# Keys and values of the last two heads as pairs, normalization by quarters, and decode logits at other places

## The chip, the cores and the metric

The kernel runs on one core of one Trainium2 chip. The time is the device time of one execution in microseconds; the median of several runs is compared. The core's engines are TensorE (PE: matmuls and transposes, with its weight loads as PEld), VectorE (DVE), ScalarE (ACT), GpSimd (POOL) and SyncE (SP, which here only issues DMAs). PSUM is the memory that TensorE writes, SBUF the memory that every engine reads.

## The reference, cut to what matters

One inference step of a hybrid decoder layer. 16 meta tokens and 512 prompt tokens form one sequence; 8 samples of 4 new tokens each decode against 512 cached positions.

```
h = rmsnorm(x, g_pre)                                  # 560 rows of 2048
q, k, v, ga, cb, cc, ch, gc, ma, mc = split(h @ w_in)  # 12288 columns
a = stick_breaking(q, k, v) * silu(ga)                 # 8 heads of 128, strictly causal
c = cb * causal_conv(cc * ch, width 3) * silu(gc)
m = sigmoid(ma + b) * (a @ w_pa) + sigmoid(mc + b) * (c @ w_pc)
y = x + rmsnorm(m @ w_out, g_post)
# stick_breaking: z = q.k / sqrt(d) + b_h
#   A[t,s] = sigmoid(z[t,s]) * prod over s<j<t of (1 - sigmoid(z[t,j])); out = A @ v
```

All inputs and outputs are float32. Keys and values of the new tokens are outputs too.

## The kernel before, in words

**Precision.** Each float32 operand of a large product is split into two parts, `hi` (rounded to the fast format F32R) and `lo` (the rest). A product is three matmuls: hi x hi, hi x lo, lo x hi. ScalarE writes `hi` by a cast, VectorE writes `lo` by a subtraction (`w_split`, L253 and L254, for weight blocks of 128 x 1024).

**Layout.** Activations are held transposed, with channels on the partitions: `h_hi` and `h_lo` have 16 blocks of 128 channels by 560 tokens. The 560 tokens are two column halves of 280 (`HC`): a half begins with 8 meta tokens and goes on with 272 others (`HQ`).

**Start (L155 to L438).** The 560 rows arrive as five row tiles (`XT`): four of 128 rows, and one of 48 with the samples and 16 rows around them. Tile 2 has three pieces, of 16, 8 and 104 rows. `norm_stats` squares a whole tile on ScalarE with a sum (L211), then takes a logarithm and an exponential for 1/sqrt and refines it by a Newton step of five small operations. `norm_half` scales half a tile by that and by g (L220). g is broadcast over the partitions by 32 small matmuls (L187) and copied to SBUF by `g_copy` (L194). TensorE then transposes 128 x 128 blocks (L227), ScalarE casts them to `h_hi` (L235), and VectorE subtracts for `h_lo` (L239). Meanwhile the weights of the queries of heads 0 to 3 arrive in eight blocks; each is split by `q_high` (ScalarE, L323) and `q_low` (VectorE, L328). `q_chunk(c)` multiplies two channel blocks for the first 256 tokens as soon as they are there (L334), eight chunks in all; the other 296 tokens follow at once behind them (L438). Nearly everything in the start is pinned (`pin`), which keeps the order that the code has.

**Heads 0 to 3 (`head_now`).** Keys, values, and the queries of head 4 + h are projected one block of 128 columns at a time by `proj` and `gemm_into` (L269): two column halves, 16 channel blocks and three terms. `natural` transposes the result for the output. Then follows the head's attention.

**Heads 4 to 7 (`head_later`).** Keys and values are projected in the same way and put into DRAM for later.

**Pairs (`seven`, `pair`).** The remaining columns of w_in are computed in pairs of 128-column blocks, by a scheme of 7 block products instead of 8 (2 x 2 blocks: channel halves by column blocks; and channel halves by token halves). It needs sums of token blocks, `t_hi` and `t_lo`, which are made once from `h_hi` and `h_lo` behind head 7 (L959 to L979). Block (0, 1) of `h` is overwritten by such a sum, so that this step must come after the last direct projection. Four pairs of attention gates come first, then convolution pairs, then 16 pairs of merge gates.

**Decode attention (`decode_steps`).** This is a generator that is advanced by `dec_step` between other work. The first part is the logits: 16 units (half of the heads, sample) of four key pages each, 16 multiply-and-sum operations on VectorE per page (L795). The first `DEC1` = 6 units run beside the heads, the others beside the pairs, where `dec_group` counts finished pairs and says how many steps follow each. Then come the weights (exponentials), and then the values (L870), from pages loaded by POOL's queue.

**Order.** The order on each engine is fixed when the program is built, by a scheduler that follows a priority by code order and its own estimate of durations, except for what is pinned. Every engine then goes through its list in order. Weights come through SP's DMA queue, with five buffers (`wraw`) and three pairs of split buffers (`whl`).

Of the kernel before, what the change touches and what calls it, by code (L numbers as in the profile page):

```python
# [9 lines left out]
F32 = mybir.dt.float32  # L10
# [7 lines left out]
P = 128  # L18
# [21 lines left out]
      (((16, "p", 256), (8, "m", 8), (104, "p", 272)), ((0, 128, HM + 256),)),  # L40
# [20 lines left out]
def hybrid_step_kernel(  # L61
# [76 lines left out]
    def rstd_of(eng, out, ss, tmp, n, w=1, later=False, fix=lambda ins: ins):  # L138

        v, r, t = (tmp[:n, i * w:(i + 1) * w] for i in range(3))  # L140
        fix(act.activation(r, ss, AF.Ln, bias=eps_c[:n], scale=1.0 / D))
        fix(act.activation(r, r, AF.Exp, scale=-0.5))

        def newton(pin=lambda ins: ins):
            pin(eng.tensor_scalar(out=v, in0=ss, scalar1=1.0 / D, scalar2=EPS, op0=ALU.mult, op1=ALU.add))
            pin(eng.tensor_mul(t, r, r))
            pin(eng.tensor_mul(t, t, v))
            pin(eng.tensor_scalar(out=t, in0=t, scalar1=-0.5, scalar2=1.5, op0=ALU.mult, op1=ALU.add))
            pin(eng.tensor_mul(out, r, t))

        if not later:
            newton()
        return newton

# [3 lines left out]
    g_bc = sp.tile([P, D], F32, name="g_bc", bufs=1)  # L158
# [5 lines left out]
    act.preload_act_table_set(LNEXP)  # L164
    def warm_up(n):

        pt = t_ps()
        for _ in range(n):
            tc.keep_in_program_order(pe.matmul(pt, lhsT=neg_one, rhs=neg_one.unsqueeze(1).broadcast_to([P, 4, P]),  # L169
                                               start=True, stop=True))  # L170
# [3 lines left out]
    g_n = sp.tile([KD, P], F32, name="g_n", bufs=1)  # L174
    act.dma_start(g_n, g_pre.rearrange("o (k p) -> (o k) p", p=P))
    g_hl = sp.tile([KD, 2, P], F32R, name="g_hl", bufs=1)
    pick = sp.tile([KD, KD], F32R, name="pick", bufs=1)
    dve.tensor_copy(pick, ident[:KD, :KD])
    dve.tensor_copy(g_hl[:, 0, :], g_n)
    dve.tensor_sub(g_hl[:, 1, :], g_n, g_hl[:, 0, :].bitcast(F32))  # L180
    g_ps = []
    for c, mk in enumerate((mm_ps, mm_ps, mm_ps, z_ps)):
        pt = mk()
        for k in range(4):
            for n in range(2):
                tc.keep_in_program_order(
                    pe.matmul(pt[:, k * P:(k + 1) * P],  # L187
                              lhsT=pick[:, 4 * c + k:4 * c + k + 1].broadcast_to([KD, P]),
                              rhs=g_hl[:, n, :], start=(n == 0), stop=(n == 1)))
        g_ps.append(pt)  # L190

    def g_copy(c):
        copy = dve.tensor_copy if c < 2 else act.copy
        pin(copy(g_bc[:, c * 512:(c + 1) * 512], g_ps[c]))  # L194

    start_ps = cycle((z_ps, z_ps, z_ps, t_ps, o_ps))

    def x_load(i):
        n = sum(r[0] for r in XT[i][0])
        xt = sp.tile([P, D], F32, name="xt", bufs=3)[:n]  # L200
        load_x(xt, i)
        return i, n, xt

    def norm_stats(x, eng=dve):

        i, n, xt = x
        ss = sp.tile([P, 1], F32, name="ss", bufs=5)[:n]
        sq = sp.tile([P, D], F32, name="sq", bufs=1)[:n]
        rs = sp.tile([P, 1], F32, name="rs", bufs=5)[:n]
        tmp = sp.tile([P, 4], F32, name="rtmp", bufs=5)  # L210
        pin(act.activation(sq, xt, AF.Square, accum_out=ss))  # L211
        return (i, n, xt, rs), rstd_of(eng, rs, ss, tmp, n, later=True, fix=pin)

    def norm_half(c, x):


        i, n, xt, rs = x
        hn = sp.tile([P, D // 2], F32, name="hn", bufs=4)[:n]
        cs = slice(c * 1024, (c + 1) * 1024)
        pin(dve.scalar_tensor_tensor(out=hn, in0=xt[:, cs], scalar=rs, in1=g_bc[:n, cs],  # L220
                                     op0=ALU.mult, op1=ALU.mult))
        parts = []
        for kq in range(2):
            pt = next(start_ps)()
            pv = pt[:, :4 * n].rearrange("p (k t) -> p k t", t=n)
            for k in range(4):
                pin(pe.transpose(out=pv[:, k, :], in_=hn[:, (4 * kq + k) * P:(4 * kq + k + 1) * P],  # L227
                                 identity=ident[:n, :n]))
            k0 = 8 * c + 4 * kq
            for r0, r1, t0 in XT[i][1]:  # L230
                parts.append(((slice(None), slice(k0, k0 + 4), slice(t0, t0 + r1 - r0)), pv[:, :, r0:r1]))

        def highs():
            for dst, src in parts:
                pin(act.copy(h_hi[dst], src))  # L235
# [1311 lines left out]
```

## Time and profile before

| | |
|---|---|
| median of 3 runs | 1575.22 us (1573.78 to 1578.06) |
| the profiled execution | 1577.82 us, of which the profile's span is 1576.2 us |
| TensorE busy | 1561.8 us, 99% of the span |
| VectorE busy | 1260.8 us, 80% |
| ScalarE busy | 755.6 us, 48% |
| POOL busy | 236.3 us, 15% |
| DMA | 252.77 MB, mean 160 GB/s |

How to read the rows that follow. A row of the timeline or the chain begins with its start and its length in microseconds. "L334" is line 334 of the kernel. "mm<-h_hi,whi" names the tile written and the tiles read. "x72" is a count. A bracket at the end of a row gives the idle time of the engine before it and what ended it. Matmuls overlap, so the distance between the starts of two of them is the pace, and the length of one is longer than that.

### The profile page before, as it was taken

What the parts mean: (1) busy time and instruction counts of PE and PEld (TensorE: products, weight loads), DVE (VectorE), ACT (ScalarE), POOL (GpSimd) and SP (SyncE); (2) the same over time, 40 slices, a digit from 0 to 9 for tenths busy, and PEclk for the clock granted to TensorE, in tenths of its full rate; (3) what the DMA queues carried; (4) which work ended last, traced back from release to release, by engine and by line L of the source; (5) the groups of instructions that cost most, each with busy time, mean ns of one, the idle gap of its engine ahead of it and who ended that gap; (6) DMA issues with size and microseconds to landing.
All of it is one profiled execution on the core that took longest, in us unless ns stands there. A gap on an engine that the chain in (4) does not pass through costs nothing.

```text
span 1576.2 us, 32345 instructions
## 1 busy us (share of the span) xinstructions
PE 1561.8 (99%) x12172; PEld 1528.3 (97%) x12172; DVE 1260.8 (80%) x3567; ACT 755.6 (48%) x1345; POOL 236.3 (15%) x428
## 2 busy tenths in 40 slices
PE   9999999999999999999999999999999999999997
PEld 8999999999999999999999999898899999999997
DVE  6328999965799999999999996655678867877776
ACT  6335555434444443444444465444476734355563
POOL 1023333222011001011011113212100010000000
PEclk9999999999999999999999999999999999999999
DMA  8245655344563454545356547666596455433345
GB/s 250 73 143 175 178 165 178 117 125 130 170 189 113 144 153 143 149 135 162 106 173 187 157 143 224 185 207 219 166 292 188 140 186 167 153 107 95 101 140 189
DMA packets 300674, 252.77 MB, mean 160 GB/s; under 512 B 11521, under 2 KB 268613, under 8 KB 299701
## 3 DMA queue, kind: packets, MB, share of 16 engines
q1 hardware_dynamic: 272021, 160.45, 34.8%
q0 software_dynamic: 28368, 89.98, 17.2%
q8 instruction: 95, 1.56, 0.4%
q14 instruction: 62, 0.51, 0.1%
q10 hardware_dynamic: 128, 0.27, 0.1%
HBM read 217.95 MB, written 32.71 MB: 159 GB/s over the span
## 4 chain that ended last, share of the span: by engine, by line
PE 98%; DVE 1%; ACT 0%; issue 0%; DVEq 0%; ACTq 0%
PE mm L994 34%; PE mm L269 28%; PE o L994 25%; PE mm L334 2%; PE z L716 1%; PE o L728 1%; PE z L334 1%; PE tp L870 1%; PE z L634 1%; PE tp L519 0%; PE z L1332 0%; PE mm L187 0%; PE tp L169 0%; DVE x_n L1374 0%; PE z L227 0%; DVE hn L220 0%
## 5 line engine op out<-in xcount | busy, mean ns | idle before, releaser
L253 ACT CAST whi<-raw 128x1024 fp32r<-128x1024 f32 x247 | 259.3, 1051 | 323.1 <-PE mm L269 100.3
L254 DVE TENSOR_TENSOR wlo<-raw,whi 128x1024 fp32r<-128x1024 f32 x247 | 301.8, 1223 | 105.5 <-ACT whi L253 103.4
L994 PE MATMUL mm<-h_hi,whi 128*128 128x272 f32 (+1 forms) x1152 | 333.0, 289 | 0.0
L994 PE MATMUL mm<-h_lo,whi 128*128 128x272 f32 (+1 forms) x1152 | 332.7, 289 | 0.0
L994 PE MATMUL mm<-h_hi,wlo 128*128 128x272 f32 (+1 forms) x1152 | 331.7, 290 | 0.1
L994 PE MATMUL o<-t_hi,whi 128*128 128x272 f32 (+1 forms) x864 | 250.2, 290 | 0.0
L994 PE MATMUL o<-t_lo,whi 128*128 128x272 f32 (+1 forms) x864 | 249.9, 289 | 0.0
L994 PE MATMUL o<-t_hi,wlo 128*128 128x272 f32 (+1 forms) x864 | 249.8, 289 | 0.0
L795 DVE CUSTOM_DVE_ANT_0 junk<-kpage,qb 128x128 f32<-128x128 f32 x1024 | 245.3, 286 | 2.1 <-DMA qb<-q_scr 1.6
L994 PEld LDWEIGHTS mm<-h_hi,whi 128*128 128x128 f32 x1152 | 217.4, 189 | 6.7 <-ACT whi L253 3.4
L994 PEld LDWEIGHTS mm<-h_hi,wlo 128*128 128x128 f32 x1152 | 216.6, 189 | 1.3 <-DVE wlo L254 0.5
L994 PEld LDWEIGHTS mm<-h_lo,whi 128*128 128x128 f32 x1152 | 216.8, 188 | 0.1
L253 ACT CAST whi<-s 128x1024 fp32r<-128x1024 f32 x126 | 132.1, 1048 | 150.1 <-PE mm L994 54.2
L254 DVE TENSOR_TENSOR wlo<-s,whi 128x1024 fp32r<-128x1024 f32 x126 | 153.8, 1220 | 61.1 <-ACT whi L253 60.9
L269 PE MATMUL mm<-h_lo,whi 128*128 128x280 f32 (+1 forms) x640 | 187.6, 293 | 0.0
L269 PE MATMUL mm<-h_hi,wlo 128*128 128x280 f32 (+1 forms) x640 | 187.1, 293 | 0.0
L269 PE MATMUL mm<-h_hi,whi 128*128 128x280 f32 (+1 forms) x640 | 186.7, 292 | 0.0
L994 PEld LDWEIGHTS o<-t_hi,wlo 128*128 128x128 f32 x864 | 163.1, 189 | 0.7 <-DVE wlo L254 0.7
L994 PEld LDWEIGHTS o<-t_lo,whi 128*128 128x128 f32 x864 | 163.4, 189 | 0.0
L994 PEld LDWEIGHTS o<-t_hi,whi 128*128 128x128 f32 x864 | 163.0, 189 | 0.1
L269 PEld LDWEIGHTS mm<-h_lo,whi 128*128 128x128 f32 x640 | 120.3, 188 | 0.8
L269 PEld LDWEIGHTS mm<-h_hi,whi 128*128 128x128 f32 x640 | 120.5, 188 | 0.5
(462 smaller groups left out, 3166.7 us busy)
## 6 DMA issues: line engine op xcount, KB each, us to landing
raw<-in_w_in SPq DMA_DIRECT2D x192, 512.0 KB, 4.2
kpage<-in_cache_k POOLq DMA_DIRECT2D x64, 256.0 KB, 3.6
qb<-q_scr POOLq DMA_DIRECT2D x32, 512.0 KB, 5.7
vpage<-in_cache_v POOLq DMA_DIRECT2D x64, 256.0 KB, 5.9
raw<-in_w_out SPq DMA_DIRECT2D x32, 512.0 KB, 3.9
gate_scr<-g POOLq DMA_DIRECT2D x32, 272.0 KB, 3.3
gt<-gate_scr POOLq DMA_DIRECT2D x16, 544.0 KB, 4.6
raw<-in_w_pc SPq DMA_DIRECT2D x16, 512.0 KB, 4.5
```

Of the source, the lines that this page charges most:

```text
L253: act.copy(hi, x)
L254: low[0] = dve.tensor_sub(lo, x, hi.bitcast(F32))
L269: pe.matmul(o, lhsT=w, rhs=r[:, t0:t1], start=(k == 0 and n == 0), stop=(k == nk - 1 and n == 2))
L334: pin(pe.matmul(o, lhsT=l, rhs=r[:, k, t0:t1], start=(start and m == 0), stop=(stop and m == 2), skip_group_check=True))
L634: pe.matmul(zt[:m, c0:c0 + n], lhsT=l[:, s0:s0 + m], rhs=r[:, ts:ts + n], start=(c0 == 0 and i == 0), stop=(i == 2), skip_group_check=True)
L716: pe.matmul(o, lhsT=l, rhs=x, start=False, stop=(i == len(ops) - 1), skip_group_check=True)
L728: pe.matmul(ot[:, ts - NMETA:ts - NMETA + n], lhsT=l[:m, st, :], rhs=x[:m, c0:c0 + n], start=False, stop=(g == GROUPS[-1] and i == 2), ski ...
L795: dve.tensor_tensor_reduce(out=junk, in0=kt[:, h * P:(h + 1) * P], in1=qt[:, t, h * P:(h + 1) * P], scale=1.0, scalar=0.0, op0=ALU.mult, o ...
L870: pin(pe.matmul(po[32 * j:32 * (j + 1), :], lhsT=lhs, rhs=rhs, start=(pg == 0), stop=last and n >= len(vts) - 4, tile_position=(0, 32 * j) ...
L994: pe.matmul(o, lhsT=l[:, k, :], rhs=r, start=(start and k == 0 and m == 0), stop=(stop and k == 7 and m == 2), skip_group_check=True)
```

## The change

It has three parts.

1. **Keys and values of heads 6 and 7** are computed as two pairs by `seven`, on the full halves of 280 columns. The token sums become 280 wide and are made in steps between the four direct projections of heads 4 and 5 (`STEPS`), with VectorE's order pinned. Small copies of these two heads go to ScalarE.
2. **The start** is rewritten as a class `Rows`. Tile 0 is loaded in two halves. Squares, scalings, transposes and splits go by halves and quarters of a tile. g stays in PSUM, broadcast by 8 matmuls of 512 columns, and is read there by the scaling. Each chunk runs its three terms one after the other, with transposes of later quarters between them. All five tiles have buffers of their own. `q_low` runs on POOL. Tile 2 is loaded with its 104 rows as 96 and 8. There are more warm-up matmuls.
3. **Decode logits**: `DEC1` is 5; the key pages beside heads 0 to 3 are distributed by `PAGES`, one is ahead of head 0, and none is beside heads 4 and 5. The sample rows of the first four queries are transposed together. The small tables are loaded behind the query stores. The later decode steps come two pairs later.

```diff
-      (((16, "p", 256), (8, "m", 8), (104, "p", 272)), ((0, 128, HM + 256),)),
+      (((16, "p", 256), (8, "m", 8), (96, "p", 272), (8, "p", 368)), ((0, 128, HM + 256),)),
-DEC1 = 6
+DEC1 = 5
-WARM = 10
+WARM = 8
+SOLO = 6
...
+    g_hl = sp.tile([P, 2, 512], F32R, name="g_hl", bufs=1)
+    g_ps = [z_ps(), z_ps(), z_ps(), o_ps()]
+    for n in range(2):
+        for c, pt in enumerate(g_ps):
+            pin(pe.matmul(pt, lhsT=pick[:, c:c + 1].broadcast_to([P, P]), rhs=g_hl[:, n, :],
+                          start=(n == 0), stop=(n == 1)))
+    warm_up(7)
...
+    class Rows:                      # one row tile
+        def square(self, half):      # ScalarE, half a tile, sum into ss[:, half]
...
+        def square_on_vector(self, half):
...
+        def newton(self):            # 4 small VectorE operations
...
+        def scale(self, c):
+            self.hn[c] = hn = sp.tile([P, 512], F32, name="hn", bufs=5)[:self.n]
+            pin(dve.scalar_tensor_tensor(out=hn, in0=self.x[:, c * 512:(c + 1) * 512], scalar=self.rs,
+                                         in1=g_ps[c][:self.n], op0=ALU.mult, op1=ALU.mult))
+        def turn(self, c):           # 4 transposes into one of two PSUM tiles (flip)
...
-        pin(dve.tensor_sub(q_lo[c], q_raw[c], q_hi[c].bitcast(F32)))
+        pin(pool.tensor_sub(q_lo[c], q_raw[c], q_hi[c].bitcast(F32)))
...
+    x0.square(0)
+    x0.base()
+    x0.square(1)
+    x0.root()
+    x0.newton()
+    x1.square(0)
+    x0.scale(0)
+    x0.turn(0)
+    warm_up(9)
+    x1.square_on_vector(1)
+    q_high()
+    q_low()
+    x1.base()
+    x0.high(0)
+    x1.root()
+    x1.newton()
+    x1.scale(0)
+    x1.turn(0)
+    warm_up(2)
+    x0.low(0)
+    x0.scale(1)
+    x1.high(0)
+    x1.low(0)
...
+    q_chunk(0, ((x0.turn, 1), (x1.turn, 1),))
...
+    q_chunk(1, ((x0.turn, 2), (x1.turn, 2),))
+    x2.square(0)
+    x2.base()
+    x0.high(2)
+    x1.high(2)
...
+    q_high()
+    q_low()
+    q_load()
+    x2.square(1)
+    x2.root()
...
+    PAGES = ((2, 2, 2, 1), (1, 1, 2, 1), (1, 1, 1, 1), (1, 1, 1, 0))
...
+    def later_pair(c, h, qs=None, ready=None):
+        raws = [hp2.tile([P, T], F32, name="raw", bufs=2) for _ in range(2)]
+        seen = []
+        for m, half, b in pair(c + h * P, HC, ready):
+            act.copy(raws[m][:, NMETA + half * HQ:NMETA + (half + 1) * HQ], b[:, HM:])
+            act.copy(raws[m][:, half * HM:(half + 1) * HM], b[:, :HM])
...
-        if n <= 25:
+        if n <= 27:
             dec_step((0, 2, 2, 2)[n - 1] if n <= 4 else 1 if n <= 20 else 4, "logits")
         else:
-            dec_step(2 if n in (26, 28) else 1)
+            dec_step(2 if n <= 30 else 1)
...
-    for h in range(NOW, H):
-        head_later(h)
...
+        STEPS = (((t_sums, 0),), ((t_sums, 2), (t_parts, 0)), ((t_parts, 2), (t_sums, 4), (t_parts, 4)),
+                 ((t_sums, 6), (t_parts, 6)))
+        for i in range(len(tiles)):              # K4, V4, K5, V5
+            h = NOW + i // 2
+            if i:
+                units[i, 1] = unit(i, 1, pin)    # weight split, VectorE pinned
+            o = gemm([units[i, u] for u in range(2)], h_rhs, ALL)
+            if i + 1 == len(tiles):
+                first_ws = blocks_of(win, GATE_K + SOLO * P)
+            for step, c in STEPS[i]:             # t_sums: 6 VectorE sums; t_parts: 5 VectorE and 3 ScalarE
+                step(c)
...
+    with tc.tile_pool(name="heads2", bufs=1) as hp2:
+        qs = hp2.tile([P, H - SOLO, TS], F32, name="qs")
+        for h in range(SOLO, H):
+            pool.dma_start(qs[:, h - SOLO, :], qt_scr[h][:, PQ:TQ])
+        later_pair(GATE_K, SOLO, qs, (first_ws, first_sum))
+        later_pair(GATE_V, SOLO)
...
     hs0 = hlctx.enter_context(tc.tile_pool(name="split0", bufs=1, side="right"))
+    after = hs0.tile([P, P], F32, name="after")
+    dve.tensor_scalar_add(after, neg_u.bitcast(F32), 1.0)
```

More of the change, by code (lines that the diff above doesn't have):

```diff
@@ L136, in rstd_by_scalar @@
         pin(act.activation(out, out, AF.Copy, scale=r))
[L138 to L153, printed above, removed]
     pin = tc.keep_in_program_order
@@ L172, in hybrid_step_kernel @@
     warm_up(WARM)
[L174 to L225, printed above, removed]
-            for k in range(4):
[L227 to L234, printed above, removed]
+    pick = sp.tile([P, 4], F32R, name="pick", bufs=1)
@@ new lines, in q_chunk @@
+    def q_chunk(c, *between):
+        for m in range(3):
+            for h in range(FIRST):
+                for k in (2 * c, 2 * c + 1):
+                    hi = by_k(q_hi[k // 2])[:, k % 2, h, :]
+                    l = by_k(q_lo[k // 2])[:, k % 2, h, :] if m == 2 else hi
+                    pin(pe.matmul(q_o[h], lhsT=l, rhs=(h_lo if m == 1 else h_hi)[:, k, START[0][0]:START[0][1]],
+                                  start=(k == 0 and m == 0 and h % 2 == 0), stop=(k == KD - 1 and m == 2),
+                                  skip_group_check=True))
+            for step, *q in (between[m] if m < len(between) else ()):
+                step(*q)
@@ L394, in hybrid_step_kernel @@
+    x0.high(1)
+    x1.high(1)
+    x0.low(1)
+    x1.scale(2)
+    x1.low(1)
     q_high()
@@ new lines, in t_parts, with unit @@
+        def t_parts(c):
+            x, y = held.pop(c)
+            t_split(part(t_hi[0], c), part(t_lo[0], c), x)
+            z = tsp.tile([P, 2, HC], F32, name="z", bufs=1)
+            whole(z, c, 1, 0)
+            t_split(part(t_hi[1], c), part(t_lo[1], c), y)
+            pin(dve.tensor_sub(z, z, x))
+            t_split(part(t_hi[2], c), part(t_lo[2], c), z)
+        tiles = [c + h * P for h in range(NOW, SOLO) for c in (GATE_K, GATE_V)]
+        def unit(i, u, pin=lambda ins: ins):
+            return w_split(w_load(win_srcs(tiles[i])[u]), pin)
@@ L1011, in seven @@
         product(x, w_split(w11), rb(0, 0), True, False)
-        with behind(last):
-            dve.tensor_add(s, w21, w22)
+        if not summed:
+            with behind(last):
+                dve.tensor_add(s, w21, w22)
         product(q, w_split(s), rb(0, 1), True, False)
@@ L1037, in seven, with pair @@
         yield 1, 0, y
[L1039 to L1044 removed]
+    def pair(c, n, ready=None):
         hs = [(HC - n, HC), (T - n, T)]
```

425 lines of the change are left out of this document (240 added, 185 removed).

## The prediction

> **What bounds the kernel.** I read the page first, then TensorE's waits, then the chain that ended last, then the timelines of the first 25 us.
>
> ```profile
> span 1576.2 us, 32345 instructions
> PE 1561.8 (99%) x12172; PEld 1528.3 (97%) x12172; DVE 1260.8 (80%) x3567; ACT 755.6 (48%) x1345; POOL 236.3 (15%) x428
> DVE  6328999965799999999999996655678867877776
> ```
>
> TensorE is busy for 99% of the span. VectorE averages 80%, and its row of 40 slices has long stretches of 9. So it is the engine that could become the bound where a change adds to it.
>
> ```profile
> PE o L227 <- DVE hn L220: 2.0, 2, 1.3
> ```
>
> The longest entry among the waits of TensorE is 2.0 us, for normalized rows in the start; outside the start it waits for hardly anything. So a time changes here in two ways: by fewer or shorter matmuls, or by a start that reaches dense matmuls sooner. The chain shows both places.
>
> ```profile
> 1.36 4.63 PE tp L169 x10
> ...
> 22.95 9.30 PE mm L334 x72
> ...
> 52.13 19.87 PE z L334 x144
> ...
> 78.55 6.65 PE mm L269 x52
> ...
> 311.64 9.24 PE mm L269 x72
> ...
> 364.35 5.28 PE mm L269 x41
> 369.63 3.03 PE mm L994 x24
> ```
>
> From about 22.6 to 52.1 us run the eight chunks of the first query projections (L334), until 78.5 us their second half, then keys and values (L269). At 369.6 us begin the pairs (L994, seven products instead of eight). Seventy-two key matmuls take 9.24 us, 0.128 us each. Between 311.64 and 364.35 lie four projections: 52.7 us, which is two heads.
>
> **Part 1: keys and values of heads 6 and 7 as pairs.** One projection of one head is 2 row halves x 16 blocks x 3 terms = 96 matmuls of 280 columns. Two heads take 192. A pair by `seven` takes 7 products x 24 = 168, with the same 280 columns. Two pairs, keys and values, drop 2 x 24 = 48 matmuls: 48 x 0.128 = **6.2 us off**, and TensorE is the chain here, so all of it counts. The natural-layout transposes, the small decode products and the output DMAs stay, as many as before.
>
> What a pair needs ahead of it is the token sums (t_hi, t_lo, 280 wide instead of 274). They move from behind head 7 to beside the four direct projections of heads 4 and 5, with VectorE's order pinned.
>
> ```profile
> 297.00:311.60 14.60, 14.60 (x116) 14.29 (x115) 14.00 (x23) 5.16 (x13) 3.59 (x7) 1.00 0.50 150
> 324.75:338.38 13.63, 13.63 (x109) 13.37 (x108) 11.15 (x17) 6.45 (x13) 3.38 (x6) 1.00 0.47 144
> ```
>
> ```profile
> L976 DVE TENSOR_TENSOR x<-x,h_lo 128x548 f32<-128x548 f32 x4 | 2.9, 716 | 0.0
> ```
>
> These are windows by projection (length, then busy TensorE, weight loads, VectorE, ScalarE, POOL). VectorE was busy for 14.00 of 14.60 us and 11.15 of 13.63 us while TensorE was busy all the time, because the scheduler already ran these sums there. In the new order the heaviest of the four projections holds 16 sums and splits x 0.72 = 11.5 us and two weight splits of 1.22 us (row in part 2), 13.9 us against some 13.2 us of matmuls. The step can begin 1 to 2 us ahead, behind the last weight split of the projection before. I take 0, with ends 0 and +3 us. The small copies (`natural`) go to ScalarE there, which had 5.16 busy of 14.60; they cost nothing while that slack is there.
>
> **Part 2: the start by quarters.** Before:
>
> ```profile
> 5.91 1.91 ACT L211 ACTIVATE sq<-xt 128x2048 f32<-128x2048 f32 x1 [3.70 <-DMA xt<-in_x_prompt]
> 7.73 0.19 ACT L211 ACTIVATION_READ_ACCUMULATOR sq<-xt 128x1 f32 x1
> 7.95 0.29 ACT L141 ACTIVATE rtmp<-ss,eps_c 128x1 f32<-128x1 f32 x1
> 8.27 0.20 ACT L142 ACTIVATE rtmp<-rtmp 128x1 f32<-128x1 f32 x1
> ...
> 13.05 0.59 ACT L194 COPY g_bc<-z 128x512 f32<-128x512 f32 x1 [1.12 <-PE z L187]
> 13.53 1.92 ACT L211 ACTIVATE sq<-xt 128x2048 f32<-128x2048 f32 x1
> 16.95 1.06 ACT L323 CAST whi<-raw 128x1024 fp32r<-128x1024 f32 x1
> ```
>
> ```profile
> 10.24 0.14 DVE L145 TENSOR_SCALAR rtmp<-ss 128x1 f32<-128x1 f32 x1
> 10.87 0.16 DVE L149 TENSOR_TENSOR rs<-rtmp 128x1 f32<-128x1 f32 x1
> 13.67 1.28 DVE L220 SCALAR_TENSOR_TENSOR hn<-xt,rs,g_bc 128x1024 f32<-128x1024 f32 x1 [1.32 <-ACT g_bc L194]
> 20.49 0.68 DVE L239 TENSOR_TENSOR h_lo<-o,h_hi 128x512 fp32r<-128x512 f32 x1
> 21.69 1.22 DVE L328 TENSOR_TENSOR wlo<-raw,whi 128x1024 fp32r<-128x1024 f32 x1
> ```
>
> ```profile
> 15.91 1.06 PE L227 MATMUL tp<-ident,hn 128*128 128x128 f32 x4
> ...
> 22.60 0.56 PE L334 MATMUL mm<-h_hi,whi 128*128 128x256 f32 x1
> 24.24 0.41 PE L334 MATMUL mm<-h_lo,whi 128*128 128x256 f32 x1
> 24.45 0.35 PE L334 MATMUL mm<-h_hi,wlo 128*128 128x256 f32 x1
> 24.64 0.28 PE L334 MATMUL mm<-h_hi,whi 128*128 128x256 f32 x1
> 24.76 0.28 PE L334 MATMUL mm<-h_lo,whi 128*128 128x256 f32 x1
> 32.09 0.60 PE L227 MATMUL tp<-ident,hn 128*128 128x128 f32 x4
> 32.52 0.60 PE L227 MATMUL o<-ident,hn 128*128 128x128 f32 x4
> ```
>
> The second tile's square starts only at 13.53 because ScalarE has the copies of g in front of it (13.05), and 1.32 us of VectorE wait for them too. In the new code these copies are gone: `scale` reads g from PSUM. Also gone are the whole-tile steps: the first chunk needs one quarter of two tiles.
>
> ```profile
> 6.00:8.00 2.00, 2.00 (x10) 2.00 (x10) 0.07 (x1) 1.97 (x3) 0.00 (x0) 1.00 0.96 402
> 12.00:14.00 2.00, 2.00 (x10) 1.88 (x10) 0.68 (x2) 0.95 (x2) 0.00 (x0) 1.00 0.85 147
> 14.00:16.00 2.00, 1.90 (x10) 1.50 (x9) 1.11 (x2) 1.94 (x4) 0.00 (x0) 1.00 0.86 201
> ```
>
> The last column of these windows is GB/s. At 402 GB/s a tile of 1.05 MB takes 2.6 us: tile 0 is there at 5.9 us (the ACT row), so tile 1 at about 8.5 and the first query weights at 9.8. New chain for the first chunk, each step by its row:
> - tile 0: second half square 0.96 + 0.19 to 7.1; logarithm and exponential 0.52 (7.95 to 8.47) to 7.6; four small VectorE steps 0.65 to 8.3; a quarter scaled, 0.68, to 9.0; four transposes 0.43 (32.09 to 32.52) to 9.4, if the warm-ups are through.
> - tile 1, in ScalarE's pinned order: half square 8.5 to 9.65, weight cast 1.06 to 10.7, tile 0's cast 0.6 to 11.3, logarithm and exponential to 11.8, small steps to 12.5, scaling to 13.2, transposes to 13.6, cast 0.6 to **14.2**. Its other half square runs on VectorE beside that, about 1.22 us for 1024 elements.
>
> The warm-ups can delay this: 8 + 8 for g + 7, all 512 wide, at 0.46 us (10 in 4.63) end at 12.0 us. Then tile 0 is cast 2.4 us later, and the first chunk starts at 16.7. The pace halves within the old first chunk: steps of 0.21 us until 24.6, then 0.12 us; at the double pace the warm-ups end near 10 us. I take 15.0 for the first chunk, against 22.6.
>
> The Trainium skill, page "TensorE: Matmul & The Clock Gate", section "What's actually happening", says that a clock gate opens after one busy window of about 3.4 us. The trace agrees in the step at 24.6 us; by that rule 10 us of unbroken wide matmuls open it in time, and the first chunk would start near 14.3 us, 0.7 us better than my sum.
>
> Chunks after that, per engine:
> - TensorE: 192 matmuls x 0.12 = 23.0, and 18 groups of four transposes x 0.43 = 7.7: 30.7 us.
> - ScalarE: 7 weight casts x 1.06, 18 casts x 0.6, 6 half squares x 1.15, three roots x 0.52: 26.7 us.
> - VectorE: 18 lows and 18 scalings x 0.68, three roots x 0.65: 26.4 us.
>
> TensorE leads, the others run at 85%, so I add 1.3 us for hand-offs: 32 us, end at 47.0 against 52.1, **5.1 us off**. Best end 14.2 + 30.7: 7.2 off. Worst: 16.7, and ScalarE's lump ahead of the third chunk (two half squares, two casts, a weight cast, a root: 5.1 us) uncovered, 52.5: 0.4 us on.
>
> The third tile as 96 + 8 rows instead of 104: at 12 to 16 us the queue moved 147 and 201 GB/s with its engines 85% busy, when by the order of issue the 104 rows were what was left. Cost or gain on the path: 0, since in the new order that tile is squared only near 18 us, and even the old rate brings 1.05 MB in 7 us. If it came late, each us would be a us on chunk 3.
>
> The low halves of the query weights go from VectorE (1.22 us) to POOL. No row shows a two-input POOL operation of that size. The nearest:
>
> ```profile
> L646 POOL TENSOR_SCALAR_AFFINE_SELECT e<-e 128x128 f32<-128x128 f32 x12 | 3.8, 337 | 14.5 <-ACT e L722 14.4
> L814 POOL TENSOR_SCALAR_AFFINE_SELECT dS<-dS 32x256 f32<-32x256 f32 x1 | 1.9, 1932 | 10.6 <-DVE dS L489 10.6
> ```
>
> Per element these give 2.6 and 7.5 ns, for 1024 elements 2.7 and 7.7 us; VectorE's 1.22 is the lower end. I take 2.7 (all 128 partitions, most instances). A chunk lasts about 3.9 us, so it is hidden.
>
> The Trainium skill speaks against this step: "GPSIMD Engine Reference", section "Elementwise — side-by-side cycle accounting", has a two-input add of 2048 elements at 4497 ns against 2293 on VectorE. An estimate from that page is 2.3 us here, by which it is still hidden and the sum stays.
>
> **Part 3: decode logits.** Twenty key pages instead of 24 run beside heads 0 to 3, one of them ahead of head 0, and 44 instead of 40 beside gates and convolutions.
>
> ```profile
> L795 DVE CUSTOM_DVE_ANT_0 junk<-kpage,qb 128x128 f32<-128x128 f32 x1024 | 245.3, 286 | 2.1 <-DMA qb<-q_scr 1.6 <-DVE z_all L795 0.4
> ```
>
> A page is 16 of these, 16 x 0.286 = 4.6 us of VectorE without the reads of the accumulator. Four pages are over 18 us, into slices where VectorE shows 9 and TensorE does not wait. The logits therefore end later, and the last value matmuls come after the last gate pair instead of one pair earlier. TensorE's work is the same. The price is head 4's split, which takes room that the value pages free. I take +0.5 us, ends 0 and +4, covered by the first w_pc products. POOL's queue gets the small tables behind the query stores. The first to be needed is the bias of head 0's decode logits, behind 96 key matmuls, 12 us later, so they cost nothing. One transpose replaces four: 0.3 us off.
>
> **Sum.** -6.2 - 5.1 - 0.3 + 0 + 0.5 = **-11 us**. The profiled run took 1577.82 us (span 1576.2), 2.6 above the median of 1575.22 (runs 1573.78 to 1578.06), so it becomes about 1566.8, and the median **1564**.
>
> **Rivals.**
> - The start gives nothing (the warm-ups at slow pace and the lump above, +0.4): only the pairs pay, -5.6: 1569.6. For it: three engines near 85% in a hand-written order. Against: the old chain's 1.32 and 1.12 us of waits for g go away for certain. 0.14.
> - More than the sum: gate open early, no hand-off loss, -13 to -16: 1559 to 1562 or a little below. 0.14.
> - The gain is handed back: VectorE's pinned sums (+3), the late value pages (+4) and half the start lost: -11 + 9.5, about 1573. VectorE's slices of 9 speak for it; TensorE's lack of waits there against. 0.10.
> - Slower: POOL's weight lows. Eight in a row from 10.7 us at 7.7 us each end at 72, the stage at 73.5 instead of 52.1: +21 - 6 = +15, 1590. It decides from about 6.4 us each (10.7 + 8 x 6.4 + 1 = 63, that is 52.1 + 6 + 4.7). 0.06.
>
> My forecast (1562 to 1568) has 0.56. The bound for no change is 0.3%, 4.7 us. Faster 0.56 + 0.14 + 0.14 = 0.84, same 0.10, slower 0.06. The range leaves out the last rival, most of the fourth and the tail of the third: 1558 to 1571.
>
> **What would show it.** Right: first L334 product at 14 to 17 us, the z products from 47, the first key product at 73 instead of 78.5; two pairs of 168 with 280 columns ahead of the first gate pair, that pair at 358 to 360 us; no new TensorE wait over 1 us. Wrong: POOL rows of the weight lows over 4 us; TensorE waiting for wlo in heads 4 and 5, or for the split of head 4 after the last gate pair.

## The result and the profile after

The changed kernel takes 1585.09 us (median of 5 runs, 1584.21 to 1587.74) against 1575.22 us before: ratio 1.0069, interval 1.0057 to 1.0081. The forecast was 1564. It is 10 us slower, and 21 us from the forecast.

The page of the changed kernel, its own execution 1584.95 us:

```profile
span 1583.4 us, 32301 instructions
PE 1554.7 (98%) x12113; PEld 1518.6 (96%) x12113; DVE 1267.8 (80%) x3582; ACT 762.8 (48%) x1372; POOL 259.1 (16%) x428
DVE  6349897676799999999999999755668867877776
```

TensorE is busy for 7 us less, yet the span is 7 us longer: 14 us of idle time are new. VectorE's row has changed where the change worked: 7 and 6 in slices 7 and 8 (238 to 317 us), where there were 9s. An engine with less in its row can be the one that the others wait for.

TensorE's waits after (what waits, for what; total, times, longest):

```profile
PE mm L263 <- DVE wlo L248: 4.5, 2, 3.0
PE tp L223 <- DVE hn L215: 3.9, 1, 3.9
PE tp L537 <- ACT nat L535: 3.1, 2, 2.7
PE z L743 <- ACT hiA L523: 1.8, 1, 1.8
```

Only the second lies in the start; outside it TensorE waited for hardly anything before. The first is the one that the prediction named as the sign of its being wrong; 3.0 of its 4.5 us lie in heads 4 and 5.

The chain that ended last, after:

```profile
4.79 13.87 DMA xt<-in_x_prompt
18.74 9.73 DMA raw<-in_w_in
...
49.87 19.63 PE z L328 x144
...
101.33 4.00 DMA qb<-q_scr
124.03 5.70 DMA qb<-q_scr
154.44 6.96 DMA qb<-q_scr
...
300.68 14.31 PE mm L263 x91
```

Three places stand out. In the start the chain follows loads of rows and of weights until 28.5 us; the chain of before had none there. Loads of `qb` (the decode queries, broadcast) are on the chain three times, and never in the chain of before. And 91 matmuls take 14.31 us at 300 us, 0.157 each, where 0.128 is the pace.

From the timelines I took the starts of the same products in every kernel: the first key product, head 4's keys (96 products each, so they can be counted), the first merged gate pair, the end. The stages between, in us:

| | to first key | heads 0 to 3 | head 4's keys to first gate pair | rest of the span |
|---|---|---|---|---|
| before (profile shown) | 78.4 | 180.5 | 110.6 | 1206.7 |
| after | 75.9 | 186.0 | 115.0 | 1206.6 |
| forecast | 73.3 | 180.2 | 104.4 | 1207.2 |

So the loss is in two stages: 5.5 us in heads 0 to 3, and 4.4 in the stage that holds the pairs, where 6.2 were to be gained. The rest of the span is the same to 0.2 us.

**Heads 0 to 3.** Timeline of POOL, VectorE and TensorE of the changed kernel at 100 us:

```profile
101.33 2.18 POOL L825 DMA_DIRECT2D qb<-q_scr  x3 [4.56 <-issue]
105.46 0.29 DVE L834 CUSTOM_DVE_ANT_0 junk<-kpage,qb 128x128 f32<-128x128 f32 x1 [7.94 <-DMA qb<-q_scr]
106.31 1.22 DVE L248 TENSOR_TENSOR wlo<-raw,whi 128x1024 fp32r<-128x1024 f32 x1
107.59 0.40 PE L263 MATMUL mm<-h_hi,wlo 128*128 128x272 f32 x1 [1.55 <-DVE wlo L248]
```

VectorE stands idle for 7.94 us before the first logit, whose queries come at 105.4. The weight low that TensorE needs is behind that logit in VectorE's list, and TensorE waits 1.55 us for it. With four more waits, TensorE loses 4.8 us in this stage; in a second profile of before (below) there is no such wait. Between the last store of these queries (96.3 us) and their broadcast (101.3) the chain follows POOL's queue, which reads page numbers (L809).

**Heads 4 and 5.** Timeline of ScalarE and VectorE, and then two windows (TensorE's busy time stands behind the length, its granted clock ahead of the last two numbers):

```profile
293.97 0.58 ACT L774 COPY qr<-o 128x512 f32<-128x512 f32 x1 [1.82 <-PE o L755]
294.45 0.66 ACT L1025 CAST t_hi<-x 128x560 fp32r<-128x560 f32 x1
295.14 0.74 DVE L1026 TENSOR_TENSOR t_lo<-x,t_hi 128x560 fp32r<-128x560 f32 x1 [4.12 <-ACT t_hi L1025]
299.41 2.35 DVE L248 TENSOR_TENSOR wlo<-raw,whi 128x1024 fp32r<-128x1024 f32 x2
328.38 1.22 DVE L1083 TENSOR_TENSOR s<-raw 128x1024 f32<-128x1024 f32 x1
```

```profile
296.00:300.00 4.00, 0.39 (x2) 0.10 (x2) 3.09 (x5) 2.24 (x6) 2.28 (x4) 0.88 0.38 129
300.00:304.00 4.00, 3.32 (x14) 3.32 (x15) 4.00 (x6) 0.00 (x0) 1.26 (x3) 0.50 0.75 212
```

The first cast into `t_hi` runs right behind the last copy of head 3's attention (L774): by the code these tiles lie where that attention had its own, and in every run with the token sums here, at 291 to 304 us, the first cast follows that copy within 0.5 us. (That the memory is the reason is read from this; other memory for the tiles wasn't tried.) VectorE, in its written-out order, waits for that cast; behind it stand four more sums and lows, and only then the weight lows that TensorE needs. TensorE then comes back at half clock. And the sum for the key pair's second product (L1083), last in that order, runs only at 328.

### The profile page after: what moved, and what is told of

The parts are those of the page before. It is cut to its first block, busy times and chain, and to the rows that moved or that the text cites. A ratio compares the mean times of both kernels' runs of the same rounds, so it can differ in the third digit from the quotient of the medians.

```text
span 1583.4 us, 32301 instructions
## 1 busy us (share of the span) xinstructions
PE 1554.7 (98%) x12113; PEld 1518.6 (96%) x12113; DVE 1267.8 (80%) x3582; ACT 762.8 (48%) x1372; POOL 259.1 (16%) x428
## 4 chain that ended last, share of the span: by engine, by line
PE 88%; DVE 4%; DMA 3%; issue 2%; ACT 1%; POOL 1%; POOLq 1%; SPq 0%; DVEq 0%; ACTq 0%
PE mm L1106 35%; PE o L1106 26%; PE mm L263 19%; PE z L328 1%; PE tp L909 1%; PE o L755 1%; PE z L743 1%; DVE junk L834 1%; DMA qb<-q_scr 1%; DMA xt<-in_x_prompt 1%; POOLq L809 1%; PE z L661 1%; DVE wlo L248 1%; DMA raw<-in_w_in 1%; PE mm L340 1%
## 5 line engine op out<-in xcount | busy, mean ns | idle before, releaser
L1106 PE MATMUL mm<-h_hi,whi 128*128 128x272 f32 (+2 forms) x1216 | 352.0, 290 | 0.0
L1106 PE MATMUL mm<-h_hi,wlo 128*128 128x272 f32 (+2 forms) x1216 | 350.8, 290 | 0.8 <-DVE wlo L248 0.7
L1106 PE MATMUL mm<-h_lo,whi 128*128 128x272 f32 (+2 forms) x1216 | 351.3, 289 | 0.0
L1106 PE MATMUL o<-t_hi,wlo 128*128 128x272 f32 (+2 forms) x912 | 264.2, 290 | 0.0
L1106 PE MATMUL o<-t_hi,whi 128*128 128x272 f32 (+2 forms) x912 | 263.9, 289 | 0.0
L1106 PE MATMUL o<-t_lo,whi 128*128 128x272 f32 (+2 forms) x912 | 263.1, 288 | 0.0
L834 DVE CUSTOM_DVE_ANT_0 junk<-kpage,qb 128x128 f32<-128x128 f32 x1024 | 242.5, 282 | 12.5 <-DMA qb<-q_scr 12.5
L1106 PEld LDWEIGHTS mm<-h_hi,whi 128*128 128x128 f32 x1216 | 229.6, 189 | 5.2 <-issue 2.5
L1106 PEld LDWEIGHTS mm<-h_hi,wlo 128*128 128x128 f32 x1216 | 228.6, 189 | 2.0 <-DVE wlo L248 1.8
L1106 PEld LDWEIGHTS mm<-h_lo,whi 128*128 128x128 f32 x1216 | 228.9, 188 | 1.0 <-issue 0.8
L1106 PEld LDWEIGHTS o<-t_hi,wlo 128*128 128x128 f32 x912 | 171.5, 188 | 0.9 <-DVE wlo L248 0.9
L1106 PEld LDWEIGHTS o<-t_hi,whi 128*128 128x128 f32 x912 | 171.7, 188 | 0.1
L1106 PEld LDWEIGHTS o<-t_lo,whi 128*128 128x128 f32 x912 | 171.8, 188 | 0.0
L263 PEld LDWEIGHTS mm<-h_hi,wlo 128*128 128x128 f32 x512 | 97.4, 190 | 5.3 <-DVE wlo L248 5.0
L263 PE MATMUL mm<-c_hl,whi 128*128 128x272 f32 x512 | 100.7, 289 | 0.0
```

What stands on the lines that cost most here:

```text
L263: pe.matmul(o, lhsT=w, rhs=r[:, t0:t1], start=(k == 0 and n == 0), stop=(k == nk - 1 and n == 2))
L834: dve.tensor_tensor_reduce(out=junk, in0=kt[:, h * P:(h + 1) * P], in1=qt[:, t, h * P:(h + 1) * P], scale=1.0, scalar=0.0, op0=ALU.mult, o ...
L1106: pe.matmul(o, lhsT=l[:, k, :], rhs=r, start=(start and k == 0 and m == 0), stop=(stop and k == 7 and m == 2), skip_group_check=True)
```

## The experiments

**The order, the place of the sums, the pages, the start.** First four runs, each one edit.

`e1`: all `pin(...)` in the stretch of heads 4 and 5 taken off.

> The changed kernel with the written-out VectorE order of the heads 4 and 5 stretch taken off (the token sums, their lows and the weight lows go where the scheduler puts them); nothing else differs. Theory A (order): in heads 4 and 5 the weight low waits behind token-sum work that itself waits for memory of head 3's attention, which costs about 11 us there (24 us for the third projection instead of 13); without the order the weight low goes ahead, the four direct projections of heads 4 and 5 take 13 to 16 us each, and the time is 1575 to 1579. Theory B (memory on ScalarE): the casts into the token-sum tiles still hold ScalarE's copies behind them, so only the 3 us wait for the weight low goes, and the time is 1580 to 1583. Theory C (the loss is elsewhere, the early pages or the pairs): 1584 to 1586.

Measured: 1576.18 us, ratio to before 1.0004 (0.9995 to 1.0013): 8.9 us better than the changed kernel. Theory A as to the order. The stage from head 4's keys to the first gate pair went from 115.0 to 106.9. The memory is not tested by this run, since the first cast still comes right behind head 3's last copy.

```diff
-        STEPS = (((t_sums, 0),), ((t_sums, 2), (t_parts, 0)), ((t_parts, 2), (t_sums, 4), (t_parts, 4)),
-                 ((t_sums, 6), (t_parts, 6)))
+        STEPS = (((t_sums, 0),), ((t_sums, 2),), ((t_parts, 0), (t_parts, 2), (t_sums, 4)),
+                 ((t_parts, 4), (t_sums, 6), (t_parts, 6)))
```

> The changed kernel with the splits of the token sums one projection later: none stands behind head 4's value projection, two behind head 5's keys, two behind head 5's values; the written-out order stays. Theory A (the order behind memory that head 3 frees late): by then that memory is free, no wait of 3 us for the weight low is left at 297 to 301 us, and the time is 1574 to 1579; theory B (the loss is the amount of VectorE and ScalarE work in this stretch, not its place): the wait moves to the last two projections, two splits of them being more work in less time, and the time is 1583 to 1590. Theory C (the loss is elsewhere): 1584 to 1586.

Measured: 1586.76 us, 1.0069 (1.0055 to 1.0082). Theory A's time fell, B's range held: the stage takes 115.4. But the condition of theory A was not met, as the timeline of ScalarE and VectorE shows:

```profile
298.41 0.66 ACT L1025 CAST t_hi<-x 128x560 fp32r<-128x560 f32 x1
299.10 0.74 DVE L1026 TENSOR_TENSOR t_lo<-x,t_hi 128x560 fp32r<-128x560 f32 x1 [5.55 <-ACT t_hi L1025]
```

The first cast still follows head 3's last copy (297.92), and VectorE still waits for it. TensorE's wait of 3.0 us at 300 us is gone, and the loss is later: from the key pair's first product to the value pair's it takes 45 us, where the changed kernel takes 36 and a fed pair 24.

```diff
-    PAGES = ((2, 2, 2, 1), (1, 1, 2, 1), (1, 1, 1, 1), (1, 1, 1, 0))
+    PAGES = ((0, 1, 2, 2), (1, 1, 2, 2), (1, 1, 2, 1), (1, 1, 1, 1))
...
-    dec_step(1, "part")
     np_ = nctx.enter_context(tc.tile_pool(name="now", bufs=2))
```

> The changed kernel with the key pages of heads 0 to 3 later: none ahead of head 0 and 5, 6, 6 and 4 beside heads 0 to 3, instead of 1 ahead and 7, 5, 4 and 3. Theory A (VectorE in its order waits for the broadcast query loads, with the weight lows queued behind them): heads 0 to 3 lost 5.4 us that way; the waits of 12.5 us for these loads shrink to 2 us or less, and the time is 1579 to 1582. Rival (the loss of heads 0 to 3 comes from the moved table loads and query transposes, or from the pages' amount): the waits go and the time stays at 1584 to 1586. Second rival: pages later run into the first solo projections and cost there what they save: 1584 to 1588.

Measured: 1579.68 us, 1.0025 (1.0016 to 1.0035): 5.4 us better. Heads 0 to 3 take 179.8 us instead of 186.0. VectorE's group of logits in this run, with its idle time at the end:

```profile
L834 DVE CUSTOM_DVE_ANT_0 junk<-kpage,qb 128x128 f32<-128x128 f32 x1024 | 245.5, 289 | 1.6 <-DMA qb<-q_scr 1.3
```

In the changed kernel that idle time was 12.5 us. TensorE waits for nothing over 0.3 us in heads 0 to 3 any more. Theory A. That the medians differ by just the 5.4 us expected is partly luck: the stage gained 6.2 us, and the profiled execution, 1.5 us above the median, gave some back elsewhere. The tables behind the query stores are still there, so they are not the cause.

`e4`: before, with the new start alone.

> The kernel before with the new start alone (normalization by quarters, the third row tile as 96 and 8 rows); decode pages and heads 4 to 7 as before. If the start gives what the changed kernel's marks show, the first key projection begins 2.5 us earlier and the time is 1572 to 1573.5. The forecast had 5.1 us: 1570. Rival (its extra POOL and VectorE work is paid back in heads 0 to 3, where the changed kernel lost 5.4 us): 1575 to 1580.

Measured: 1575.15 us, 0.9998 (0.9989 to 1.0007), although its first key product is at 75.9 us and its span is 1573.4. The start gains nothing in the median and 2.5 us against the profile of before. Both cannot be right, unless that profile is not typical. The rival's range holds the time, but not its reason: heads 0 to 3 take 180.5 us here, as before.

**A second profile of before.** No edit.

> The kernel before, unchanged, for a second profile of it: the profile shown was of an execution of 1577.8 us, 2.6 above the median, and the new start alone moved the median by -0.2 although its first key projection began 2.5 us earlier than in that profile. Theory A (the profile shown had a late start): an execution near 1575 begins its first key projection at 76 us, as the new start does, and the new start is worth nothing. Theory B (the start is worth 2.5 us and the new start gives it back later): an execution near 1575 begins it at 78 us and is shorter in a later stage.

Measured: 1575.32 us; its profiled execution took 1575.35, with the first key product at 76.0 us and later stages of 180.5, 110.6 and 1206.7. Theory A. TensorE's broadcasts of g and first chunk in this run, and then the same broadcasts in the profile of before that the prediction used:

```profile
5.92 2.89 PE L187 MATMUL mm<-g_hl,pick 16*128 16x128 f32 x24
19.57 0.56 PE L334 MATMUL mm<-h_hi,whi 128*128 128x256 f32 x1
```

```profile
5.92 5.38 PE L187 MATMUL mm<-g_hl,pick 16*128 16x128 f32 x24
```

The same 24 small matmuls took 2.89 us here and 5.38 there. Here TensorE reached its full pace at 6 us, though it lost it again from 9 to 23 us; in the execution of the profile shown it did not reach it until 24.6, and the first chunk came at 22.6 instead of 19.57. Of its 2.6 us above the median 2.4 were in the start. Of the 26 runs of before beside the first four experiments, 20 lie at 1573.9 to 1575.8 us and 6 at 1577.5 to 1578.2. The six have a mean granted clock of 0.997 or 0.998, as the profile shown (0.998), and the twenty 0.993 to 0.996, as this one (0.993). So the early start is the usual one.

The recorded clock has to be read with care there: the late start has the higher one. One window of this run, and the same of the profile shown:

```profile
10.00:12.00 2.00, 1.18 (x6) 1.21 (x7) 1.92 (x2) 1.98 (x2) 0.00 (x0) 0.50 1.23 432
10.00:12.00 2.00, 2.00 (x12) 2.00 (x11) 1.86 (x7) 0.59 (x1) 0.00 (x0) 1.00 1.13 428
```

The second says 1.00 while eight small matmuls took 1.90 us, the slow pace.

**Both mends.** `e5` joins the edits of `e1` and `e3`.

> The changed kernel with both mends: no written-out VectorE order in heads 4 and 5, and the key pages of heads 0 to 3 later. If the two losses are separate, they add: 1585.1 - 8.9 - 5.4 = 1570.8, so 1569 to 1572.5; heads 0 to 3 take 180 us as in the late-pages run, the stretch from head 4's keys to the first gate pair 107 us as in the run without the order. Against the run with the new start alone (1575.2) this is then the worth of the pairs: 4.4 us of the 6.2 forecast. Rival: both mends free the same VectorE time, and the sum is 1573 to 1577.

Measured: 1572.52 us, 0.9981 (0.9972 to 0.9990). Heads 0 to 3: 179.8; head 4's keys to the first gate pair: 108.0. The losses add up, nearly (1570.8 expected; the result lies between the two ranges). The stage of the pairs is 2.6 us shorter than before, not 6.2. The value pair takes 23.6 us, two direct projections 26.3, so it saves its 2.7; the key pair takes 26.3 and saves nothing: TensorE waits 1.7 and 0.4 us there for weight casts, and its granted clock is 0.68 from 324 to 328 us.

**The start.** Edits on top of `e5`:

```diff
     x0.turn(0)
-    warm_up(9)
+    warm_up(23)
```

> As the kernel with both mends, with 23 instead of 9 warm-up products between the transposes of the first two row tiles. Theory A (the clock): TensorE's 3.9 us of idleness at 11.8 us lowers its granted clock to 0.50 and 0.71 in the two following windows of 2 us; with the gap filled by 14 products of 0.26 us the clock stays at 1.00, the first eight products of the chunk take 1.0 instead of 1.9 us, and the first key projection begins 1 to 2 us earlier, as does the end. Rival (weights and VectorE set the chunks): the clock stays and the first key projection does not move by more than 0.5 us.

Measured: 1570.72 us, 0.9969 (0.9958 to 0.9980), first key product 1.3 us earlier than in `e5`. Theory A. What it mended, in the changed kernel (windows, then the timeline of TensorE, VectorE and POOL):

```profile
14.00:16.00 2.00, 0.26 (x1) 0.26 (x2) 1.90 (x5) 0.00 (x0) 0.51 (x1) 0.93 0.97 242
16.00:18.00 2.00, 2.00 (x8) 1.46 (x8) 1.43 (x3) 1.10 (x2) 0.00 (x0) 0.50 0.99 227
18.00:20.00 2.00, 2.00 (x15) 2.00 (x15) 1.51 (x3) 0.49 (x2) 1.50 (x1) 0.71 1.12 222
```

```profile
15.74 1.12 PE L223 MATMUL tp<-ident,hn 128*128 128x128 f32 x4 [3.92 <-DVE hn L215]
17.53 1.93 PE L340 MATMUL mm<-h_hi,whi 128*128 128x256 f32 x8
13.03 1.50 DVE L209 SCALAR_TENSOR_TENSOR w<-w,w 128x1 f32<-128x1 f32 x1 [1.70 <-ACT w L203]
12.17 2.34 POOL L321 TENSOR_TENSOR wlo<-raw,whi 128x1024 fp32r<-128x1024 f32 x1 [9.28 <-ACT whi L316]
```

and in `e6`:

```profile
16.00:18.00 2.00, 1.79 (x13) 1.36 (x12) 1.89 (x4) 1.53 (x2) 0.03 (x1) 1.00 1.01 165
```

```profile
17.00 1.21 PE L340 MATMUL mm<-h_hi,whi 128*128 128x256 f32 x8 [0.21 <-ACT h_hi L231]
```

After 3.92 us of idleness the granted clock is 0.50 and then 0.71, and eight products take 1.93 us. With the gap filled the clock is 1.00 and they take 1.21.

```diff
-    warm_up(9)
+    warm_up(15)
     x1.square_on_vector(1)
-    q_high()
-    q_low()
     x1.base()
-    x0.high(0)
     x1.root()
     x1.newton()
+    q_high()
+    q_low()
+    x0.high(0)
```

> As the kernel with both mends, with the second row tile's root and its Newton step ahead of the first weight cast on ScalarE and the first weight low on POOL, and 15 warm-up products. Theory A (ScalarE's order and a VectorE instruction of 1.50 us beside POOL's low): the Newton instruction goes from 13.0 to 11.6 us and takes 0.2 us, the second tile's transposes begin 2.7 us earlier at 13 us, the clock stays above 0.9, and the first key projection and the end come 2 to 3 us earlier. Rival (the loads set the chunks): the transposes move and the first key projection moves by less than 0.7 us.

Measured: 1568.83 us, 0.9965 (0.9951 to 0.9979), with the first key product at 74.0, 1.9 us earlier than in `e5`: just short of theory A's 2 to 3, and far from the rival's 0.7.

```profile
11.61 0.22 DVE L209 SCALAR_TENSOR_TENSOR w<-w,w 128x1 f32<-128x1 f32 x1 [0.35 <-ACT w L203]
14.39 1.22 PE L340 MATMUL mm<-h_hi,whi 128*128 128x256 f32 x8 [0.21 <-ACT h_hi L231]
```

The first chunk is 3.1 us earlier than in the changed kernel (14.39 against 17.53), the first key product 1.9. The rest goes to later chunks: from the first product to the other half they take 33.3 us instead of 32.1, and the chain there follows loads until 30.4 us. Whether the loads are the next limit was not tried.

**Can the key pair have its time back?** Edits on top of `e7`. To compare with, the windows at the key pair in two profiles of `e7` itself (the second is `e7_again`, below):

```profile
320.00:324.00 4.00, 3.15 (x22) 2.94 (x23) 3.62 (x4) 2.80 (x4) 0.74 (x2) 1.00 0.53 149
320.00:324.00 4.00, 3.24 (x14) 3.05 (x15) 3.71 (x4) 2.71 (x4) 0.65 (x2) 0.65 0.52 147
```

TensorE waits the same 1.7 and 0.4 us in both; the granted clock stayed at 1.00 in the first and fell to 0.65 in the second, and the key pair took 24.9 and 26.4 us. So some 1.5 us of its loss is the clock behind the waits, which comes in one execution and not in another.

```diff
-                k_out(hp, h, raw, qs_all[:, h, :], act.copy)
+                k_out(hp, h, raw, qs_all[:, h, :])
...
-                v_store(h, v_out(hp, h, raw, act.copy))
+                v_store(h, v_out(hp, h, raw))
```

> As the kernel with both mends and the reordered start (1568.8), with the copies of the key and value transposes of heads 4 and 5 on VectorE instead of ScalarE (4 heads' tiles by 1.09 us). Theory A (ScalarE's queue): in the run with both mends the key pair takes 26.3 us and the value pair 23.6, because the second and third sums' weight casts stand behind token-sum casts and copies on ScalarE (waits of 1.7 and 0.4 us for them); 4.4 us less on ScalarE brings the casts forward, the key pair takes 24 to 25 us and the time is 1566.5 to 1568. Rival (VectorE is as full: it works without a gap from 300 to 327 us): its lows come later instead, and the time is 1569 to 1572.

Measured: 1572.03 us, 0.9975 (0.9966 to 0.9985), the key pair 26.0 us at a granted clock of 1.00, where `e7` took 24.9. No gain, the rival; the waits become 1.5 and 0.4 us for casts and 0.9 for a low.

`e9`: `t_split` of the third sum and of the difference casts by `pool.tensor_copy`.

> As the kernel with both mends and the reordered start (1568.8), with a third of the token-sum casts (those of the third sum and of the difference, 8 of 16, 0.57 us apart on ScalarE) on POOL, which has 11 us of work in the 40 us there. Theory A (ScalarE's queue holds the key pair's weight casts): 4.5 us leave ScalarE, the waits of the key pair go, it takes 23.6 us instead of 26.3 and the time is 1566 to 1567. Rival (a cast on POOL takes over 1.3 us beside VectorE, by its lows of 2.38 us for 1024 columns, and the lows behind it wait): 1569 to 1575.

Measured: 1572.56 us, 0.9977 (0.9967 to 0.9988), the key pair 27.3 us. The rival: TensorE now waits for a low of the difference (`h_lo`) behind a POOL cast.

```profile
PE mm L1105 <- DVE h_lo L1025: 2.9, 1, 2.9
```

`e13`: in `whole`, `dve.tensor_add` becomes `pool.tensor_add`.

> As the kernel with both mends and the reordered start (1568.8), with the 16 additions of high and low parts of the token sums on POOL instead of VectorE (0.66 us each there, 10.6 us in all, of which some 7 lie after 294 us). Theory A (VectorE, which works without a gap from 300 to 327 us, is what the key pair waits for): the key pair takes 24 us instead of 26 and the time is 1566 to 1567.5. Rival (on POOL an addition takes 1.3 us or more by its lows, and the sums that need them come later): 1569 to 1574.

Measured: 1580.12 us, 1.0035 (1.0023 to 1.0047). Worse than the rival: the stage takes 118.2 us. Groups of POOL and VectorE from 260 and 280 to 345 us:

```profile
L1039 POOL TENSOR_TENSOR z<-h_hi,h_lo 128x560 f32<-128x560 f32 x4 | 7.5, 1880 | 1.3 <-DVE t_lo L1025 1.3
```

```profile
L1025 DVE TENSOR_TENSOR t_lo<-x,t_hi 128x560 fp32r<-128x560 f32 x4 | 4.1, 1031 | 2.5 <-ACT t_hi L1024 2.5
L1047 DVE TENSOR_TENSOR r<-y,r 128x560 f32<-128x560 f32 x2 | 3.9, 1926 | 0.0
```

An addition takes 1.88 us on POOL, where the lows' 2.34 us for 1024 columns would give 1.3 for 560, and VectorE's own operations beside it take 1.03 and 1.93 us instead of 0.73. Neither engine works at its own pace.

**Which part of the order?** The changed kernel, with only some instructions taken out of the written-out order of VectorE. First the weight lows of heads 4 and 5:

```diff
-                units[i, 1] = unit(i, 1, pin)
+                units[i, 1] = unit(i, 1)
...
-                units[i + 1, 0] = unit(i + 1, 0, pin)
+                units[i + 1, 0] = unit(i + 1, 0)
```

> The changed kernel with only the weight lows of heads 4 and 5 taken out of the written-out VectorE order; the token sums, their lows and the rest of that order stay. Theory A (the loss is the weight low standing behind token-sum work that waits): 1575.5 to 1577.5, all that the run without any order brought. Rival (the token sums' own order, which waits for casts and delays the pair's first weights): only the 3 to 4 us of the wait at 297 us go, and the time is 1580 to 1583.

Measured: 1586.72 us, 1.0066 (1.0052 to 1.0080). Theory A fell, and the rival's time too: the wait in heads 4 and 5 goes, and the time stays. TensorE's waits from 250 to 345 us, and VectorE's sum for the key pair:

```profile
PE mm L1106 <- ACT whi L247: 4.3, 1, 4.3
PE mm L1106 <- DVE wlo L248: 3.0, 1, 3.0
```

```profile
327.81 1.22 DVE L1083 TENSOR_TENSOR s<-raw 128x1024 f32<-128x1024 f32 x1
```

The waits are new ones, in the key pair (L1106), for the cast and the low of that sum. Then only that sum:

```diff
-                pin(dve.tensor_add(first_sum, first_ws[1], first_ws[2]))
+                dve.tensor_add(first_sum, first_ws[1], first_ws[2])
```

> The changed kernel with only the first weight sum of the key pair taken out of the written-out VectorE order (it stands last in it and ran at 328 us); weight lows and token sums keep it. Theory A (that sum is what sets the pair: its casts and lows follow at 330 to 340 us, whatever was waited for before): the sum runs before 320 us and the time is 1576 to 1580. Theory B (the weight lows and that sum stand behind the same token work, and freeing one leaves the other): 1583 to 1587.

Measured: 1588.71 us, 1.0081 (1.0068 to 1.0094), with the sum at 307 us. Theory A fell; B held, with a time 1.7 us above its range. TensorE's waits from 285 to 345 us:

```profile
PE mm L263 <- DVE wlo L248: 3.9, 2, 3.0
PE tp L537 <- ACT nat L535: 3.3, 2, 2.7
```

`e11`: both.

> The changed kernel with the weight lows of heads 4 and 5 and the first weight sum of the key pair out of the written-out order; only the token sums and their lows keep it. Theories A and B both: 1575.5 to 1578, as without any order (1576.2). Theory C (the token sums' own order, which waits for ScalarE's casts, holds the pair's products): 1581 to 1587.

Measured: 1578.74 us, 1.0021 (1.0012 to 1.0030). In the same stretch only this is left:

```profile
PE o L1106 <- ACT whi L247: 1.6, 1, 1.6
PE mm L1106 <- ACT whi L247: 0.4, 1, 0.4
```

| taken out of the order | median | head 4's keys to first gate pair | heads 0 to 3 |
|---|---|---|---|
| nothing (after) | 1585.1 | 115.0 | 186.0 |
| weight lows | 1586.7 | 114.5 | 186.7 |
| the key pair's sum | 1588.7 | 116.5 | 186.1 |
| both | 1578.7 | 106.2 | 188.4 |
| everything | 1576.2 | 106.9 | 184.4 |

Theory B: either alone brings nothing, both bring 8.8 us in that stage. The token sums' own order, still kept in `e11`, costs nothing there. (All five keep the early pages, and heads 0 to 3 vary by 4 us among them, where every build with the later pages takes 179.8; that puts `e11` 0.7 us above its range, and it is the difference of the last two medians.)

**The best version again.**

> The kernel with both mends and the reordered start once more, beside the others: 1568 to 1570.

Measured: 1571.43 us, 0.9972 (0.9960 to 0.9983). It missed its range by 1.4 us, but the intervals of the two comparisons overlap: this kernel is 0.3% faster than before, 4 to 6 us. In its two profiles the stage of the pairs has 4.0 and 2.5 us of that, the reordered start 2.0 and 2.1, and heads 0 to 3 0.7.

## Why the prediction was wrong, step by step

- **"Token sums: I take 0, ends 0 and +3."** This step failed, by some 8 us. It compared amounts: 13.9 us of VectorE work against 13.2 us of matmuls in the heaviest projection. It did not ask from when the token tiles may be written, which is 294 us, when head 3's attention frees their memory, nor who stands behind them in VectorE's order. Two things did, the weight lows and the key pair's first sum, and either, left there, costs the whole loss. (The order is shown by `e1`, `e10`, `e11` and `e12`; the memory is a reading of the timelines, and `e2` did not test it.) The windows that were quoted, VectorE busy for 14.00 of 14.60 us with no wait of TensorE, showed a scheduler that placed the sums by itself; they say nothing of the same work in a written order.
- **Part 1, 6.2 us off by 48 matmuls.** The mechanism is right: a pair takes 23.6 us for 26.3 where it is fed. The key pair was not: with both mends 2.6 us of the 6.2 were left, and 4.0 and 2.5 in the two profiles with the reordered start (106.6 and 108.1 us against 110.6). The most was 4.4, in `e11`. (In `e1` the key pair took 23.4 us, but the four projections ahead of it took 1.8 more than in `e5`.) What holds its weights stays open: less work on ScalarE (`e8`) did not mend it, and less on VectorE was not had, since POOL slowed VectorE down.
- **Part 3, key pages that "run beside heads 0 to 3"** at no cost. This step failed, by 5.5 us. It priced the pages' amount of VectorE time. What counted was that the first logit's queries must go to memory (stores issued from 94.8 us) and come back broadcast (issued at 101.3, there at 105.4), and that a weight low was queued behind it. Before, the first broadcast was issued only at 119.8 us, and no logit of heads 0 to 3 waited for one.
- **Part 2, 5.1 us off.** This step failed: nothing came of it. Half was the basis: the profile's start was 2.4 us later than in a usual execution. Half was the first chunk, at 17.5 us and not 15.0 (14.2 by the prediction's chain). That chain had ScalarE's order right, the second tile's root behind a weight cast and a cast of tile 0; three terms were too small. The second tile's square began at 9.74 us, when its load was there, and not at 8.5. Its Newton step took 1.50 us instead of 0.22 beside POOL's low. And its four transposes took 1.12 us, where the sum had 0.43, behind a gap of 3.92 us that lowered the clock. These are 1.2, 1.3 and 0.7 of the 3.3 us; `e7` mended the last two by another order and more warm-ups. Full pace had come in time, as hoped: the seven warm-ups at 7.04 us took 1.77 us, 0.25 each instead of 0.46. But the step at 24.6 us bears out no rule for when it opens: in the same execution TensorE ran almost without a gap from 1.36 to 17 us and stayed slow. The length of the chunks was right: 32.1 us from the first product to the other half, 32 forecast, but a usual execution of before takes 29.9, so the start that begins 2 us earlier ends at the same time.
- **POOL's weight lows**, 2.7 us taken: 2.34 to 2.41 measured, hidden but for that Newton step. The estimate of 2.3 us from the Trainium skill ("GPSIMD Engine Reference", section "Elementwise — side-by-side cycle accounting") was the better one, and the slower rival that rested on 7.7 us is out.
- **Late value pages, +0.5:** nothing; the rest of the span is 1206.6 against 1206.7 us. The last value matmuls did move behind the last pair.
- **The rivals.** "VectorE's pinned sums" stood in one at +3, with 0.10 together with two other mishaps. It came at nearly three times that price, and should have been a rival on the slower side by itself; the early pages stood in none.

In sum, against the second profile of before: -0.1 for the start, +5.5 for the pages, +4.4 for the stage of the pairs, -0.1 for the rest: +9.6 in the spans, and +9.9 in the medians.

## What to carry to other kernels

Before work is moved in a fixed order, write for each instruction the time from which its inputs and its memory are there, and then the list of what stands behind it; busy shares show neither. A wait that goes away proves nothing until the time moves: of two instructions in the same queue each can hide the other, and only taking out both shows the cost. Take a second profile of the kernel before when the first lies above the median, and see in which stage the difference is.

## What the runs showed of the hardware

- A VectorE operation with two SBUF inputs waits for a POOL operation that reads SBUF: the Newton step on one column began at 13.03 us and ended at 14.53, POOL's low ended at 14.51. In `e13` such pairs took 1.93 instead of 0.73 us. The Trainium skill, page "SBUF — State Buffer", section "SBUF: two separate sides", says that such operations of the two engines lock each other out for a whole instruction; the trace agrees.
- A wait of TensorE can cost its clock as well: after 3.92 us without matmuls it was granted 0.50, and in heads 4 and 5, after two waits of 2.7 and 3.0 us, 0.50 over 4 us. After 1.7 and 0.4 us it stayed at 1.00 in one execution of `e7` and fell to 0.65 in the other. And in `c1_before` it was 0.50 from 10 to 22 us though no wait there was over 0.8 us, so length alone does not decide it.
- The same 24 matmuls in the same kernel took 2.89 or 5.38 us, by whether full pace had come by 6 us; with the later pace the first key product came 2.4 us later. The recorded clock was 1.00 in that late start.
